# Sixteen stores taken off the load queue of a pooling and memory-attention layer: eight issued by POOL, eight by ACT

## The chip, the cores and the metric

The kernel runs on one core of one Trainium2 chip. The metric is the device time of one execution in microseconds (us). The engines of the core are PE (matrix products), DVE (vector), ACT (scalar functions), POOL (general purpose) and SP, which computes nothing and only issues transfers. ACT and POOL can issue transfers too. Each engine works through its own list of instructions strictly in order; engines wait for one another, and for transfers, by semaphores.

## The reference

One layer of a streaming encoder on 2048 tokens of width 1024, in float32:

```python
hn = rms_norm(h, norm_g[i])
mem_kv = jnp.einsum('bnd,de->bne', mem_n, w_mem_kv[i])
proj = jnp.einsum('bsd,de->bse', hn, pool_w_in[j])
u, mq, gate = jnp.split(proj, [POOL_WIDTH, POOL_WIDTH + MEM_WIDTH], axis=-1)
tok = multi_scale_pool(u, pool_w_group[j], pool_scale[j])      # windows 2, 4, 8, 16; then a 192x192 product per group
mem_o = memory_attention(mq, mem_k, mem_v)                     # 4 heads of 64, 256 memory rows
branch = jnp.concatenate([tok, mem_o], axis=-1) * jax.nn.silu(gate)
h = h + jnp.einsum('bse,ed->bsd', branch, w_out[i])
return rms_norm(h, final_norm_g)
```

## The kernel before, in words

Every float32 product is made of three products of a high and a low half: `_split` (L42 to L46) writes the high half by a cast (L38, mostly on ACT) and the low half by a subtraction (L46, on DVE), and `_mm3` issues the three matmuls (L51, L52, L53). A tile of weights can't be used by PE before both of its halves are made.

The 2048 tokens are four blocks of 512, taken as two pairs. For the first pair the input projection runs over tiles of 128 columns: `q` tiles (queries of the memory attention), `g` tiles (gates) and `z` tiles (pooling inputs), in the order of the list `TILES`. It begins with four query products, then gate tile 5. Between the products stand hooks: the fold (`fold`, hook 12), the loads and products of the memory keys and values (`load_memory`, `memory`), the row statistics of the second pair (`row_stats`), and four stages (`stage`) that prepare the second pair's inputs. Eighteen steps of the attention (`Attention.step`: scores L580 and L581, softmax L583 to L592, transposes L603, mix L615) are spread over the same stretch.

The fold multiplies the pooling weights into the input weights: for each of 8 row blocks k it loads 384 KB (`w_uT`, tile `raw`), PE makes the product, ACT copies it out of PSUM (L322) into a tile `zz`, and one transfer stores it to `w_z` in DRAM (L323), from where the `z` tiles are loaded later. `raw` tiles rotate through 4 buffers, `zz` tiles through 4.

`take_query` scales and splits each query product into `zz` and stores the two halves to `q_d` (L488); for the first pair that is 4 products with 2 stores each. `take_gate` puts a gate through Silu (L497) and stores it to `g_d`; ACT issues that store itself (L498).

All loads up to the second pair go through `load`, which keeps them in one order on SP:

```python
    def load(**kw):

        if not last:
            last.append(sp.dma_start(**kw))
        else:
            with tc.issue_after(last[-1].ins):
                last.append(sp.dma_start(**kw))
```

The order of each engine's list is worked out by a scheduler from a timeline of its own, so a store that moves to another engine can move other instructions as well. Transfers issued by SP and ACT take eight completion semaphores in turn (DMAHW0 to DMAHW7 in the lists below). A transfer may only be issued when the transfer that had its semaphore before it has landed; if it has not, the issuing engine stands still, and everything behind it on that engine too. Transfers issued by POOL have eight of their own (DMASW0 to DMASW7).

Of the kernel before, what the change touches and what calls it, by code (L numbers as in the profile page):

```python
# [8 lines left out]
F32 = mybir.dt.float32  # L9
# [32 lines left out]
def _split(nc, hi, lo, src, hi_eng, lo_eng="dve"):  # L42

    _cast(nc, hi_eng, hi, src)
    e = nc.gpsimd if lo_eng == "pool" else nc.vector
    return e.tensor_tensor(out=lo, in0=src, in1=hi.bitcast(F32), op=ALU.subtract)  # L46


def _mm3(nc, ps, ahi, alo, bhi, blo, start, stop, **kw):

    nc.tensor.matmul(ps, lhsT=ahi, rhs=bhi, start=start, stop=False, **kw)  # L51
    nc.tensor.matmul(ps, lhsT=ahi, rhs=blo, start=False, stop=False, **kw)  # L52
    nc.tensor.matmul(ps, lhsT=alo, rhs=bhi, start=False, stop=stop, **kw)  # L53
# [3 lines left out]
def trunk(ctx, tc, x, xT, mem, memT, norm_g, mem_norm_g, w_mem, w_out, w_in, w_uT, w_g, p_scale, final_g,  # L57
# [4 lines left out]
    nc = tc.nc  # L62
    sp = nc.sync
# [16 lines left out]
    def raw_tile(shape=(P, D)):  # L80
        return raw.tile(list(shape), F32, name="raw")
# [4 lines left out]
    def zz(shape, dt=F32):  # L86

        n = 1
        for v in shape[1:]:
            n *= v  # L90
        t = zw.tile([P, HALO + D], dt, name="zz")[:, :n]
        if len(shape) == 3:
            t = t.rearrange("p (a b) -> p a b", a=shape[1])
        return t
# [22 lines left out]
# [7 lines that stand above are left out]
        return last[-1]  # L124
# [170 lines left out]
    w_z = dram.tile([NJ, P, KT, P], F32, name="w_z")  # L295

    def fold():

        low = att.tile([P, D], F32R, name="ptl", bufs=1)[:, :4 * GD].rearrange("p (a l e) -> p a l e", a=2, l=2)
        tails = [[att.tile([P, 2, GD], F32R, name="pr") for _ in range(2)], [low[:, a] for a in range(2)]]  # L300
        for t in tails[0] + tails[1]:
            nc.vector.memset(t.bitcast(F32), 0.0)
        for l in range(2):
            r = slice(64 * l, 64 * l + 64)
            for a in range(2):
                _split(nc, tails[0][a][r, l, :], tails[1][a][r, l, :], wgb[r, a, :], "dve")
        for k in range(KT):
            wu = raw_tile((P, 6, P))
            load(out=wu, in_=w_uT[k])
            zs = zz((P, 6 * P))  # L310
            ut = ch.tile([P, 2, 2, P], F32R, name=("wh", "wl")[k % 2])
            nc.scalar.copy(ut[:, 0], wu[:, 4:6, :])
            nc.gpsimd.tensor_tensor(out=ut[:, 1], in0=wu[:, 4:6, :], in1=ut[:, 0].bitcast(F32), op=ALU.subtract)
            pss = [ps_mm.tile([P, 2, GD], F32, name="mm") for _ in range(2)]
            for a, ps in enumerate(pss):
                for l in range(2):
                    nc.tensor.matmul(ps[:, l, :], lhsT=wu[:, 2 * a + l, :], rhs=wga[:, 2 * a + l, :], start=l == 0,  # L317
                                     stop=False)
                _mm3(nc, ps, ut[:, 0, a, :], ut[:, 1, a, :], tails[0][a], tails[1][a], False, True)
            for a, ps in enumerate(pss):  # L320
                c = slice(2 * a * GD, 2 * (a + 1) * GD)
                nc.scalar.copy(zs[:, c], ps.rearrange("p l e -> p (l e)"))  # L322
            sp.dma_start(out=w_z[:, :, k, :].rearrange("j p f -> p j f"), in_=zs.rearrange("p (j f) -> p j f", j=6))  # L323

# [88 lines left out]
    q_d = [dram.tile([2, 2, P, 2, BT], F32, name=f"q_d{s}") for s in range(2)]  # L415
# [62 lines left out]
    def take_query(s, p0):  # L478
        def take(i, a, ps, op, rest):
            p = p0 + i  # L480
            src = ps
            if rest is not None:
                src = sgp.tile([P, BT], F32, name="sg")
                nc.vector.tensor_tensor(out=src, in0=ps, in1=rest, op=op)
            q = zz((P, 2, BT), F32R)
            _split(nc, q[:, 0, :], q[:, 1, :], src, "act")
            for i in range(2):
                sp.dma_start(out=q_d[s][p, i, :, a, :], in_=q[:, i, :].bitcast(F32))  # L488
        return take

    def take_gate(s, j):
# [278 lines left out]
    def norm(a):  # L770
        first_norm(a)
        for f in unscaled[a]:
            f()

    hooks = {7: [lambda: norm(0)], 10: [lambda: norm(1)], 12: [fold, lambda: ahead.append(load_tile(w_in[6], load)), lambda: loaded.extend(load_memory())],
             14: [lambda: load_memory_rest(loaded)],
             15: [lambda: memory_norm(loaded)], 17: [lambda: memory(loaded)], 19: [lambda: stats(0)], 21: [lambda: stats(1)]}
# [97 lines left out]
```

## Time and profile before

| | |
|---|---|
| time, median of 3 executions | 634.14 us (634.12 to 636.33) |
| time of the profiled execution | 636.03 us |
| span of the profiled execution, first to last instruction | 634.3 us |
| PE busy | 598.7 us, 94% of the span |
| DVE, ACT, POOL busy | 406.2, 324.9, 153.7 us |
| moved by the transfers | 124.41 MB, mean 196 GB/s |

The span is the part of the time that the trace divides among instructions; the profiled execution spent 1.7 us around it. PE is busy in all but some 36 us, so only what changes those, or the clock at which PE runs, can change the time by much.

### The profile page before, as it was taken

The page shows a single profiled execution, that of the slowest core. Times are in us where ns is not written, and L with a number is a line of the kernel's source. Part 1 is how long each engine was busy: PE and PEld are TensorE (multiplying, and loading weights), DVE is VectorE, ACT ScalarE, POOL GpSimd, SP SyncE. Part 2 cuts the span into 40 slices and gives each one's busy share as a digit, 9 for nine tenths or more (in the row PEclk, how much of TensorE's full clock was granted, in tenths as well). Part 3 has the DMA queues.
Part 4 walks back from the last instruction along what each step waited for, and adds up shares of the span by engine and source line. Part 5 has one row for each costly group of instructions (what it writes and reads, how often), then busy time and mean ns, then how long its engine had stood idle before and what let it go on. Part 6 is the DMA issues. An engine that isn't in the chain of part 4 may idle for free.

```text
span 634.3 us, 8389 instructions
## 1 busy us (share of the span) xinstructions
PE 598.7 (94%) x2846; PEld 496.6 (78%) x2846; DVE 406.2 (64%) x686; ACT 324.9 (51%) x672; POOL 153.7 (24%) x165
## 2 busy tenths in 40 slices
PE   7989779989989999999999999999999999999992
PEld 4879668868767888888888777877888888888882
DVE  6370247599785768896779756999864257515126
ACT  6825446346463664665864889644734234114112
POOL 0021123253451304100049200454000002107016
PEclk9999979989989999999999999999999999999997
DMA  8949995466464943667233434277991256940006
GB/s 315 398 158 337 395 352 158 116 208 216 158 240 149 314 152 124 224 218 238 92 101 97 168 110 144 60 231 252 389 405 63 65 187 218 359 167 0 1 0 265
DMA packets 54382, 124.41 MB, mean 196 GB/s; under 512 B 6722, under 2 KB 15682, under 8 KB 54340
## 3 DMA queue, kind: packets, MB, share of 16 engines
q1 hardware_dynamic: 45972, 106.57, 48.9%
q10 hardware_dynamic: 6832, 12.60, 5.3%
q0 software_dynamic: 1536, 4.72, 2.0%
q8 instruction: 22, 0.36, 0.2%
q14 instruction: 20, 0.16, 0.1%
HBM read 86.63 MB, written 36.70 MB: 194 GB/s over the span
## 4 chain that ended last, share of the span: by engine, by line
PE 62%; DVE 14%; DMA 7%; ACT 6%; POOL 5%; issue 4%; SPq 1%; ACTq 0%; POOLq 0%; DVEq 0%
PE mm L51 14%; PE mm L52 14%; PE mm L53 14%; POOL zz L522 4%; DMA raw<-in_xT 3%; PE sc L52 2%; PE sc L53 2%; PE pt L52 2%; PE pt L53 2%; PE pt L51 2%; PE sc L51 2%; DVE wl L46 2%; PE mm L317 2%; DVE raw L101 2%; DVE zz L531 1%
## 5 line engine op out<-in xcount | busy, mean ns | idle before, releaser
L51 PE MATMUL mm<-x,wh 128*128 128x512 f32 x480 | 190.9, 399 | 13.2 <-ACT wh L38 8.3
L52 PE MATMUL mm<-x,wh 128*128 128x512 f32 x480 | 189.5, 395 | 0.6 <-DVE x L229 0.6
L53 PE MATMUL mm<-x,wl 128*128 128x512 f32 x480 | 187.2, 394 | 0.0
L46 DVE TENSOR_TENSOR wl<-raw,wh 128x512 fp32r<-128x512 f32 x104 | 76.7, 741 | 110.8 <-ACT wh L38 110.5
L38 ACT CAST wh<-raw 128x512 fp32r<-128x512 f32 x104 | 63.7, 618 | 113.2 <-PE pt L53 80.5
L522 POOL TENSOR_TENSOR zz<-zz 128x527 f32<-128x527 f32 (+6 forms) x64 | 84.5, 1332 | 145.7 <-DVE zz L549 48.7
L51 PEld LDWEIGHTS mm<-x,wh 128*128 128x128 f32 x480 | 91.3, 190 | 34.5 <-ACT wh L38 9.2
L52 PEld LDWEIGHTS mm<-x,wh 128*128 128x128 f32 x480 | 91.2, 190 | 18.8 <-DVE x L229 1.2
L53 PEld LDWEIGHTS mm<-x,wl 128*128 128x128 f32 x480 | 91.1, 190 | 18.1
L51 PE MATMUL mm<-wh,x 128*128 128x512 f32 x128 | 49.7, 390 | 0.4 <-ACT sg L497 0.4
L53 PE MATMUL mm<-wh,x 128*128 128x512 f32 x128 | 49.8, 389 | 0.0
L52 PE MATMUL mm<-wl,x 128*128 128x512 f32 x128 | 49.8, 389 | 0.0
L674 POOL TENSOR_TENSOR rstdo<-sso,half 128x1 f32<-128x1 f32 x16 | 14.7, 919 | 129.5 <-DVE sso L716 129.5
L587 ACT ACTIVATE pr<-sc,nm 128x256 f32<-128x256 f32 x64 | 29.8, 471 | 24.9 <-DVE nm L583 23.0
L592 ACT ACTIVATE pr<-pr,rc 128x256 f32<-128x256 f32 x64 | 29.1, 504 | 19.9 <-DVE rc L590 19.2
L51 PEld LDWEIGHTS mm<-wh,x 128*128 128x128 f32 x128 | 24.0, 188 | 5.8 <-ACT sg L497 0.8
L53 PEld LDWEIGHTS mm<-wh,x 128*128 128x128 f32 x128 | 24.0, 188 | 5.0
L38 ACT CAST x<-raw 128x512 fp32r<-128x512 f32 x28 | 16.8, 619 | 21.7 <-DVE raw L266 13.9
L52 PEld LDWEIGHTS mm<-wl,x 128*128 128x128 f32 x128 | 24.0, 188 | 5.0
L46 DVE TENSOR_TENSOR x<-raw,x 128x512 fp32r<-128x512 f32 x28 | 23.6, 864 | 4.1 <-ACT x L38 3.9
L38 ACT CAST x<-zz 128x512 fp32r<-128x512 f32 x32 | 18.3, 618 | 13.5 <-DMA zz<-br_d 5.2
L583 DVE TENSOR_REDUCE nm<-sc 128x2 f32<-128x512 f32 x32 | 21.8, 682 | 5.2 <-PE sc L581 5.0
(180 smaller groups left out, 1049.8 us busy)
## 6 DMA issues: line engine op xcount, KB each, us to landing
raw<-in_w_in SPq DMA_DIRECT2D x19, 512.0 KB, 5.1
x<-in_x SPq DMA_DIRECT2D x16, 512.0 KB, 8.6
g_d<-sg ACTq DMA_DIRECT2D x32, 256.0 KB, 2.7
raw<-in_w_out SPq DMA_DIRECT2D x16, 512.0 KB, 4.5
raw<-w_z SPq DMA_DIRECT2D x12, 512.0 KB, 4.3
sg<-g_d SPq DMA_DIRECT2D x24, 256.0 KB, 3.7
br_d<-zz SPq DMA_DIRECT2D x12, 512.0 KB, 4.4
x<-in_xT SPq DMA_DIRECT2D x8, 512.0 KB, 7.7
```

Of the source, the lines that this page charges most:

```text
L38: return nc.scalar.copy(hi, src)
L46: return e.tensor_tensor(out=lo, in0=src, in1=hi.bitcast(F32), op=ALU.subtract)
L51: nc.tensor.matmul(ps, lhsT=ahi, rhs=bhi, start=start, stop=False, **kw)
L52: nc.tensor.matmul(ps, lhsT=ahi, rhs=blo, start=False, stop=False, **kw)
L53: nc.tensor.matmul(ps, lhsT=alo, rhs=bhi, start=False, stop=stop, **kw)
L101: return eng.tensor_tensor(out=o, in0=a, in1=b, op=ALU.subtract)
L317: nc.tensor.matmul(ps[:, l, :], lhsT=wu[:, 2 * a + l, :], rhs=wga[:, 2 * a + l, :], start=l == 0, stop=False)
L522: nc.gpsimd.tensor_tensor(out=cur[rows, c0:c1], in0=prev[rows, c0:c1], in1=prev[rows, c0 - step:c1 - step], op=ALU.add)
L583: nc.vector.tensor_reduce(out=nm, in_=ps, axis=AX.X, op=ALU.max, negate=True)
L587: nc.scalar.activation(out=pr[:, h, :], in_=ps[:, h, :], func=AF.Exp, bias=nm[:, h:h + 1], accum_out=su[:, h:h + 1])
L592: nc.scalar.mul(pr[:, h, :], pr[:, h, :], rc[:, h:h + 1])
L674: nc.gpsimd.tensor_tensor(out=ro, in0=sso[:, 1, t:t + 1], in1=half[:, :1], op=ALU.pow)
```

## The change

The stores of the fold (L323) are issued by ACT, and the query stores of the first pair (L488) by POOL. Both were issued by SP. The query stores of the second pair stay on SP.

```diff
@@ -320,7 +320,7 @@
             for a, ps in enumerate(pss):
                 c = slice(2 * a * GD, 2 * (a + 1) * GD)
                 nc.scalar.copy(zs[:, c], ps.rearrange("p l e -> p (l e)"))
-            sp.dma_start(out=w_z[:, :, k, :].rearrange("j p f -> p j f"), in_=zs.rearrange("p (j f) -> p j f", j=6))
+            nc.scalar.dma_start(out=w_z[:, :, k, :].rearrange("j p f -> p j f"), in_=zs.rearrange("p (j f) -> p j f", j=6))
@@ -485,7 +485,7 @@
             for i in range(2):
-                sp.dma_start(out=q_d[s][p, i, :, a, :], in_=q[:, i, :].bitcast(F32))
+                (sp if s else nc.gpsimd).dma_start(out=q_d[s][p, i, :, a, :], in_=q[:, i, :].bitcast(F32))
```

On SP, from the fourth fold load to the memory loads, the list of before was as follows (`raw<-in_w_uT` are the loads of the fold, `x_639` and `mq` take the memory, `x_644` its weights):

```order
L123 DMA raw<-in_w_uT 128x768 x4
L488 DMA q_d_174<-zz 128x512 x8
L123 DMA raw<-in_w_uT 128x768
L323 DMA w_z<-zz 128x6x128
L123 DMA raw<-in_w_uT 128x768
L323 DMA w_z<-zz 128x6x128
L123 DMA raw<-in_w_uT 128x768
L323 DMA w_z<-zz 128x6x128
L123 DMA raw<-in_w_uT 128x768
L323 DMA w_z<-zz 128x6x128
```

Of the changed kernel SP's list at that place, up to the weights of gate tile 3 (the second `raw<-in_w_in`) and the first rows for the statistics (`x_974<-in_x`), is:

```order
L123 DMA raw<-in_w_uT 128x768 x8
L123 DMA raw<-in_w_in 128x1024
L123 DMA x_639<-in_mem 128x1024 x2
L123 DMA mq<-in_memT 128x1024 x2
L123 DMA x_644<-in_w_mem 128x1024 x2
L123 DMA pth<-in_w_mem 128x1024
L123 DMA ptl<-in_w_mem 128x1024
L123 DMA raw<-in_w_in 128x1024
L123 DMA ci<-in_cinv 128x96
L123 DMA x_974<-in_x 128x1024 x2
```

Sixteen stores have left SP's list; the loads stand in the same order as before.

On ACT, between the gates of tile 4 (`sg_724` and `sg_728`) and the cast of the weights of gate tile 3 (`wh_736`), the list of before, with what each row waits for, was:

```order
L497 ACTIVATE sg_724<-sg_724 128x512 [waits DVE_49]
L368 ACTIVATE zz_753<-mq_146,gm_149 128x256 [waits DMAHW5_49,DMAHW1_49,Activation_49]
L368 ACTIVATE zz_753<-mq_146,gm_149 128x256 x3
L498 DMA g_d0_170<-sg_724 128x512 [waits DMAHW5_49,Activation_49]
L497 ACTIVATE sg_728<-sg_728 128x512 [waits DVE_49]
L498 DMA g_d0_170<-sg_728 128x512 [waits DMAHW0_49,Activation_49]
L38 CAST wh_736<-raw_732 128x512 [waits DMAHW4_49,Pool_49]
```

In the changed kernel the same place reads:

```order
L497 ACTIVATE sg_724<-sg_724 128x512 [waits DVE_49]
L498 DMA g_d0_170<-sg_724 128x512 [waits DMAHW3_49,Activation_49]
L368 ACTIVATE zz_753<-mq_146,gm_149 128x256 [waits DMAHW5_49,DMAHW1_49]
L368 ACTIVATE zz_753<-mq_146,gm_149 128x256 x3
L497 ACTIVATE sg_728<-sg_728 128x512 [waits DVE_49]
L498 DMA g_d0_170<-sg_728 128x512 [waits DMAHW7_49,Activation_49]
L38 CAST wh_736<-raw_732 128x512 [waits DMAHW4_49,Pool_49]
```

The second gate store stood behind DMAHW0 and now stands behind DMAHW7. SP's lists with their waits show who has each: in both kernels it is the second transfer of `x_974<-in_x`. The first gate store waited for the last fold store (DMAHW5) and now waits for `ptl<-in_w_mem` (DMAHW3).

The third place is on PE, at the transposes L603 of one attention step in the stretch of the stages. Of before:

```order
L615 MATMUL sc<-ptl,vhl 128x256
L52 MATMUL mm<-x_265,wh 128x512
L53 MATMUL mm<-x_264,wl 128x512
L603 MATMUL pt<-ident,pr 128x128 x4
L51 MATMUL mm<-x_176,wh 128x512
```

and of the changed kernel:

```order
L615 MATMUL sc<-ptl,vhl 128x256
L51 MATMUL mm<-x_176,wh 128x512
L52 MATMUL mm<-x_177,wh 128x512
L603 MATMUL pt<-ident,pr 128x128 x4
L53 MATMUL mm<-x_176,wl 128x512
```

These transposes stand two large matmuls further down the projection than before. Shifts of one to eleven such matmuls are found at most attention steps behind the fold.

## Rows read from the trace of the kernel before

**Rows 1.** The page's head and part 1: busy us (share of the span) xinstructions.
```profile
span 634.3 us, 8389 instructions
PE 598.7 (94%) x2846; PEld 496.6 (78%) x2846; DVE 406.2 (64%) x686; ACT 324.9 (51%) x672; POOL 153.7 (24%) x165
```

**Rows 2.** Timeline of PE, 74 to 89 us: start, us, what [idle before <-releaser].
```profile
74.82 0.39 PE L53 MATMUL mm<-x,wl 128*128 128x512 f32 x1
83.47 0.80 PE L51 MATMUL mm<-x,wh 128*128 128x512 f32 x1 [8.27 <-ACT wh L38]
```

**Rows 3.** Chain that ended last, 74 to 84 us: start, us, what.
```profile
74.29 8.01 DMA x<-in_x
...
82.38 0.33 ACTq L498
```

**Rows 4.** Timeline of ACT, 79 to 83 us.
```profile
79.77 0.33 ACTq L498 DMA_DIRECT2D g_d<-sg  x1
80.14 0.63 ACT L497 ACTIVATE sg<-sg 128x512 f32<-128x512 f32 x1 [3.05 <-DMA w_z<-zz]
...
82.80 0.62 ACT L38 CAST wh<-raw 128x512 fp32r<-128x512 f32 x1 [2.04 <-DMA x<-in_x]
```

**Rows 5.** Stretches: PE, PEld, DVE, ACT, POOL busy (xcount), PEclk, DMA share, GB/s.
```profile
39.00:45.20 6.20, 6.20 (x33) 5.28 (x32) 2.78 (x7) 0.71 (x2) 0.00 (x0) 1.00 0.11 42
46.00:64.00 18.00, 18.00 (x110) 18.00 (x109) 2.14 (x4) 10.61 (x23) 2.93 (x4) 1.00 1.03 342
64.00:75.20 11.20, 11.20 (x50) 8.95 (x48) 3.23 (x8) 5.30 (x12) 1.98 (x4) 1.00 1.06 396
75.20:82.30 7.10, 0.01 (x1) 0.00 (x0) 0.69 (x1) 2.52 (x6) 0.55 (x1) 0.70 1.05 405
83.50:88.20 4.70, 4.70 (x14) 4.02 (x15) 4.08 (x8) 4.09 (x8) 0.00 (x0) 0.50 1.01 329
```

**Rows 6.** Timeline of SP, 28 to 77 us: start, us to the end of the last issue.
```profile
33.98 13.07 SPq L488 DMA_DIRECT2D q_d<-zz  x8
47.40 0.33 SPq L123 DMA_DIRECT2D raw<-in_w_uT  x1
...
71.20 0.40 SPq L323 DMA_DIRECT2D w_z<-zz  x1
...
73.67 2.84 SPq L123 DMA_DIRECT2D x<-in_x  x4
```

**Rows 7.** What SP waited for, 30 to 98 us: total, times, longest.
```profile
SPq L323 <- ACT zz L322: 5.1, 5, 1.9
...
SPq L123 <- PE mm L317: 0.3, 1, 0.3
```

**Rows 8.** The instructions on the tile w_z, 46 to 76 us: ns min/median/max, first and last start.
```profile
L323 SPq DMA_DIRECT2D w_z<-zz x8: 370/420/1179, 49.7 to 71.2; - x8
```
**Rows 9.** Transfers issued from 46 to 82.3 us: xcount, size, median us to landing.
```profile
w_z<-zz SPq DMA_DIRECT2D x8, 384.0 KB, 7.3
```

**Rows 10.** Timeline of POOL, at the fold and at a store of 256 KB later on.
```profile
51.90 0.73 POOL L313 TENSOR_TENSOR wh<-raw,wh 128x256 fp32r<-128x256 f32 x1 [13.40 <-ACT wh L312]
...
127.47 0.61 POOL L279 DMA_DIRECT2D xs_d<-raw  x1 [0.85 <-DVE raw L266]
```

**Rows 11.** Timeline of PE: the first row behind four of its idle times, 138 to 201 us.
```profile
139.01 0.38 PE L615 MATMUL sc<-ptl,vhl 128*128 128x256 f32 x1 [2.69 <-DVE ptl L46]
...
160.74 0.39 PE L615 MATMUL sc<-ptl,vhl 128*128 128x256 f32 x1 [0.35 <-DVE ptl L46]
...
184.02 1.11 PE L603 MATMUL pt<-ident,pr 128*128 128x128 f32 x4 [2.83 <-ACT pr L592]
...
200.94 0.38 PE L615 MATMUL sc<-ptl,vhl 128*128 128x256 f32 x1 [0.93 <-DVE ptl L46]
```

**Rows 12.** Stretches behind two of them, columns as in rows 5.
```profile
139.00:142.80 3.80, 3.79 (x14) 3.31 (x15) 2.92 (x6) 1.47 (x3) 0.00 (x0) 0.56 0.81 252
...
183.80:187.20 3.40, 3.18 (x10) 2.59 (x11) 3.40 (x5) 2.98 (x6) 2.60 (x3) 0.50 0.64 167
```

## The prediction

> **What bounds the kernel now.** I began with the page: a span of 634.3 us with PE busy for 598.7 of them [rows 1]. A change of transfers can only pay where PE stands idle or runs slowly, so the next view was PE's timeline. Its longest stop lies just behind the edited code: the last matmul of gate tile 4 starts at 74.82 and takes 0.39, the next one starts at 83.47 after 8.27 us without work [rows 2]. The reader should see in that row that the releaser is ACT's cast of the weights of gate tile 3 (L38).
>
> Why is ACT late? The chain of waits [rows 3] and ACT's timeline [rows 4] answer it. ACT issued the first gate store of tile 4 at 79.77, having stood idle for most of the 3.05 us ahead of the Silu at 80.14, which the profile puts down to a store of the fold; it issued the second gate store at 82.38, and only then came the cast, at 82.80. The second gate store waited for a transfer of `x<-in_x` that was issued at 74.29 and took 8.01, so it landed at 82.30. That wait is not for data. The store reuses the completion semaphore of that transfer, as the list of ACT ahead shows.
>
> Why does that transfer land so late? The stretches [rows 5] show it: from 39 to 45.2 us the transfer engines are used to 0.11, but from 46 to 82.3 us the share is 1.03 to 1.06 in each stretch. Everything that lands in these 36 us lands when its turn comes. SP issued ahead of that all along: the fold's stores took a median of 7.3 us from issue to landing [rows 9], for 384 KB that need about 1.0 us at the 396 GB/s of 64 to 75.2 [rows 5].
>
> After the stop PE runs at a granted clock of 0.50, the 1.2 GHz level, until 88.2 [rows 5]: 4.70 us of which half, 2.35, is lost. The next idle times lie between 126 and 202 us. Those of 2.69 at 139.01 and 2.83 at 184.02 [rows 11] are followed by stretches at 0.56 and 0.50 [rows 12]; behind those of 0.35 and 0.93 the trace has no slow stretch.
>
> **The change part by part.**
>
> *Query stores leave SP.* SP spent 13.07 us, from 33.98 on, on eight of them, mostly waiting for their data, and issued the fifth fold load at 47.40 [rows 6]. It looks as if the loads could start 13 us sooner. They can't: the fifth fold load needs the `raw` buffer of the first, which PE reads only when it begins the fold, and after the query stores SP still waited 0.3 us for PE's matmul L317 [rows 7]. The compiled list of the changed kernel has the four L317 rows of a fold block ahead of its other matmuls, so the buffer comes free somewhat sooner. I allow the load 0.3 to 0.7 us; the engines are empty then (0.11), so up to that much could pass to everything behind. I take 0.3.
>
> *Query stores on POOL.* A store of 256 KB costs POOL 0.61 us at 127.47 [rows 10]; eight cost 4.9. POOL stood idle for 13.40 us before its first fold subtraction behind the fourth block, at 51.90 [rows 10], so they are hidden, the four early ones (from about 35 us) in the 10 us before PE begins the fold. Without that cover POOL's subtractions, and with them PE, would be up to 2.4 us late (four stores), which the stop at 75 would absorb.
>
> *Fold stores leave SP.* That frees eight issues of 0.42 (3.4 us [rows 8]) and 5.1 us of waiting for ACT's copies [rows 7], 8.5 us together. SP will run ahead of where it was, but it feeds a set of engines that is full. From 46 us on the bytes ahead of the transfer that ends the stop are the same ones: the fold's loads and stores, the memory, its weights, gate tile 3. The last fold store was issued at 71.20 on SP [rows 6], ahead of it already. So I take 0 for this part, with a gain of 8.27 + 2.35 = 10.6 as the far bound, if the whole stop went.
>
> The Trainium skill says the same against the change in its page DMA: Bandwidth & Descriptors, section Issuing engines are not separate DMA queues: transfers of all issuing engines run on the same 16 engines, and issuing from several only saves issue time. By that rule alone the gain would be the issue time, 3.4 us; by the shares above, it is nothing, since SP's issue time is not what the landing waits for.
>
> *Fold stores on ACT.* Eight issues at 0.33 (a gate store, [rows 4]) to 0.42 make 2.6 to 3.4 us more on ACT. ACT is busy for 10.61 of the 18 us from 46 to 64 and 5.30 of 11.2 after that [rows 5], so it has 13 us of room, and PE's products have four PSUM buffers. ACT may also stand still for a semaphore: the sixth store waits for the weights of tile 4 to land, which the cast behind it needs anyway. I take 0. If the cover fails, PE's fold or gate tile 4 slips; PE has to wait until 83 all the same, so the first 8 us of that cost nothing.
>
> *What the stop waits for afterwards.* ACT's list still has the second gate store ahead of the cast, and it still waits for the same second `x_974` transfer. The first gate store now waits for `ptl<-in_w_mem`, four transfers earlier. It will therefore be sent sooner and share the engines with the two `x_974` transfers: 256 KB at 405 GB/s [rows 5] is up to 0.65 us. I take 0.2, since only part of it falls ahead of the landing. So PE goes on at 83.47 - 0.3 + 0.2, about 83.4.
>
> *What moves behind.* The scheduler moved the transposes and mixes of most attention steps one to eleven large matmuls down. At 184.02 the shift is two matmuls; a large one takes about 0.23 us, as 48 of them in 11.2 us show [rows 5], so that stop of 2.83 may lose 0.45; at 160.74 the mix is six further down, which covers the 0.35 [rows 11]. I take 0.5 as a gain; the order behind 200 us differs more and I give it nothing, with 1.5 either way.
>
> **The sum.** 0.1 + 0.5 = 0.6 us less: a profiled execution of 636.03 would become 635.4. That execution lies 1.9 above the median of the runs shown, 634.14; applied to the median the forecast is 633.5. I count within 0.5%, 3.2 us, as no change, which is about what a measurement of this kernel can tell.
>
> **The rivals.**
>
> A. *The loads do come forward.* For it: SP waited 5.1 us for the fold's copies, and with them gone its issues lie earlier. If the landing moved by those 5.1 us, PE would go on at 78.4. The clock of 0.70 over the 7.1 us of the stop [rows 5] says it fell for the last 4.3 of them, at about 78.0, so the slow stretch would remain: 634.14 - 5.1 = 629.0. Against it: the share of 1.03 and more from 46 us on. It decides by that share alone: if some of it is not bytes but gaps between transfers of one queue, a second queue fills them.
>
> B. *The stores on their own queue take turns with the loads.* Then the first gate store (0.65) and a fold store that still runs (384 KB at 405 GB/s, 0.97) go ahead of the `x_974` transfers: 1.6 us later, 635.2 with the gain of 0.5 behind. The Trainium skill has this rule, in the same page, section Queues, rings and completion order: each engine goes round its queues packet by packet. No row shows more than one busy queue for long here.
>
> C. *One more stop like those at 139 and 184.* An order that puts a transpose or a mix where DVE or ACT is 2.7 us behind costs 2.69 and, over the 3.80 us at 0.56 [rows 12], another 1.7: 4.4 more, 634.14 - 0.1 + 4.4 = 638.4. For it: both stops come from such an order, and a share of the rows there is new. Against: the shifts that I found lie downwards, which gives DVE and ACT more time. It decides at an idle time between 0.93, which has no slow stretch, and 2.69, which has one.
>
> D. *One of these two stops goes.* The mirror image: 184.02 loses 1.9 of its 2.83 and with it the slow stretch (half of 3.40, 1.7): 3.6, to 630.5.
>
> **Chances and range.** The forecast has 0.50, A 0.13, B 0.13, C 0.12, D 0.12. The forecast and B end within 0.5%, but the unknown order behind 200 us can carry some of them over either edge, 0.02 to each side. Faster: A, D and 0.02, with the part of A and D that stays within the bound taken off (0.02), 0.25. Slower: C and 0.02, 0.14. The same: 0.61. The range leaves out C and the deeper half of A: 628.8 to 637.0. The likeliest case has a range of its own from its bounds: 633.5 - 0.4 (the load) - 1.5 (the order) = 631.6, and 633.5 + 0.3 + 0.45 (the gate store) + 1.5 = 635.8.
>
> **What would show it.** Right: PE's stop ends between 82.5 and 84 us, with the releaser ACT L38 and ACT's second gate store waiting for `x<-in_x`; the share from 46 to 82 us is still 1.0 or more; the fold stores land in under 7.3 us; POOL's issues lie before 48 us, and none of PE's idle times names POOL there. Wrong: a stop at 75 us that is shorter than 7 us or ends with another releaser; idle time of PE between 46 and 64, which would mean that ACT's stores hold its copies up; or a changed number of stretches at half clock from 126 to 202 us, which would carry the difference in place of the stores.

## The result, and the profile after

| | before | changed |
|---|---|---|
| time, median of 4 executions each, taken together | 635.24 us (634.12 to 637.13) | 641.57 us (640.44 to 643.02) |
| ratio to before, 95% interval | 1 | 1.0102 (1.0078 to 1.0127) |
| span of the profiled execution | 634.3 us | 640.2 us |

The change makes the kernel 1.0% slower, outside the range that was forecast. The page of the changed kernel has the same work as [rows 1] but for two table loads more on ACT, some 3 us more of PE's busy time, and 3 us more in which PE stands idle:

```profile
span 640.2 us, 8398 instructions
PE 601.8 (94%) x2846; PEld 499.6 (78%) x2846; DVE 413.2 (65%) x686; ACT 327.5 (51%) x674; POOL 155.6 (24%) x173
```

PE's timeline of the changed kernel, the rows that begin behind a longer idle time (in brackets, with what ended it):

```profile
68.84 0.80 PE L51 MATMUL mm<-x,wh 128*128 128x512 f32 x1 [3.79 <-ACT wh L38]
84.07 0.50 PE L51 MATMUL mm<-x,wh 128*128 128x512 f32 x1 [2.53 <-ACT wh L38]
...
136.43 0.39 PE L615 MATMUL sc<-ptl,vhl 128*128 128x256 f32 x1 [1.61 <-DVE ptl L46]
159.61 0.39 PE L615 MATMUL sc<-ptl,vhl 128*128 128x256 f32 x1 [2.65 <-DVE ptl L46]
181.76 0.44 PE L603 MATMUL pt<-ident,pr 128*128 128x128 f32 x2 [2.05 <-ACT pr L592]
216.73 0.83 PE L603 MATMUL pt<-ident,pr 128*128 128x128 f32 x4 [1.80 <-ACT pr L592]
...
348.58 0.58 PE L615 MATMUL sc<-ptl,vhl 128*128 128x256 f32 x1 [2.36 <-DVE ptl L46]
427.19 0.80 PE L51 MATMUL mm<-x,wh 128*128 128x512 f32 x1 [2.83 <-DVE u L104]
```

The stop of 8.27 at the edited place [rows 2] is now two, 3.79 and 2.53, and those of [rows 11] have their answers at 136, 160 and 182. How the edited place divides differs between executions: three kernels further down that have the same lists up to there (two_places, three_moves, old_order_behind_600) show 1.80 and 7.42, 1.62 and 5.97, 3.50 and 3.42. What before does not have are the three last rows. Each of them is followed by a stretch at half the clock, as these windows of the changed kernel show (the column that reads 0.50 is PE's granted clock; 1.2 of 2.4 GHz):

```profile
218.84:222.25 3.41, 3.41 (x12) 2.93 (x12) 2.86 (x5) 1.48 (x3) 0.48 (x1) 0.50 0.32 126
348.54:351.95 3.41, 3.37 (x14) 3.18 (x14) 3.41 (x6) 1.79 (x4) 2.20 (x2) 0.50 0.91 287
427.05:430.46 3.41, 3.27 (x8) 2.62 (x9) 2.48 (x5) 0.00 (x0) 0.00 (x0) 0.50 0.70 243
```

To see where the time goes, the large matmuls (rows of L51 to L53 that write `mm`) are counted in PE's timeline of each kernel, and their start times compared at equal counts. The 600th starts at 206.78 before and at 202.81 in the changed kernel: up to there, the edited place included, the profiled execution of the changed kernel is 4.0 ahead. The 900th starts at 285.55 and 285.89, the 1470th at 445.42 and 451.03. So 4.3 are lost from the 600th to the 900th, where the stop at 216.73 lies, and 5.3 from the 900th to the 1470th, where the other two lie. The first loss is largely one of this execution: two_places and three_moves have the same lists up to the 900th, show 0.33 and 0.34 at the place of the stop at 216.73, and lose 1.5 and 1.3 there. No store that was moved is in either stretch.

DVE explains the last two stops. Its timeline in the changed kernel:

```profile
343.02 0.69 DVE L104 TENSOR_TENSOR u<-mm,u 128x512 f32<-128x512 f32 x1
343.62 1.39 DVE L46 TENSOR_TENSOR wl<-raw,wh 128x512 fp32r<-128x512 f32 x1
344.94 2.98 DVE L537 SCALAR_TENSOR_TENSOR zz<-zz,psc,sg 128x512 f32<-128x512 f32 x2
347.85 0.68 DVE L46 TENSOR_TENSOR ptl<-pt,pth 128x512 fp32r<-128x512 f32 x1
...
424.19 2.22 DVE L537 SCALAR_TENSOR_TENSOR zz<-zz,psc,sg 128x512 f32<-128x512 f32 x2
426.45 0.69 DVE L104 TENSOR_TENSOR u<-mm,u 128x512 f32<-128x512 f32 x1
```

and the same instructions in the kernel before:

```profile
342.72 0.68 DVE L46 TENSOR_TENSOR ptl<-pt,pth 128x512 fp32r<-128x512 f32 x1
343.32 2.39 DVE L537 SCALAR_TENSOR_TENSOR zz<-zz,psc,sg 128x512 f32<-128x512 f32 x2
...
421.88 0.69 DVE L104 TENSOR_TENSOR u<-mm,u 128x512 f32<-128x512 f32 x1
422.49 1.81 DVE L537 SCALAR_TENSOR_TENSOR zz<-zz,psc,sg 128x512 f32<-128x512 f32 x2
```

PE waits for `ptl` in the one place and for `u` in the other. Before, each stands ahead of the two pooling rows L537; in the changed kernel it stands behind them.

At the edited place the engines were as full as forecast (a share of 0.98 from 46 to 64 us, 1.00 to 75.2 and 1.01 to 83), but the landings moved apart. The transfer view of 46 to 74 us of the changed kernel (count, size, median us from issue to landing):

```profile
w_z<-zz ACTq DMA_DIRECT2D x8, 384.0 KB, 11.5
...
mq<-in_memT SPq DMA_DIRECT2D x2, 512.0 KB, 6.1
x<-in_w_mem SPq DMA_DIRECT2D x2, 512.0 KB, 6.3
```

and of the same stretch before:

```profile
w_z<-zz SPq DMA_DIRECT2D x8, 384.0 KB, 7.3
...
mq<-in_memT SPq DMA_DIRECT2D x2, 512.0 KB, 9.5
x<-in_w_mem SPq DMA_DIRECT2D x2, 512.0 KB, 10.6
```

On a queue of their own the fold's stores land later (7.3 to 11.5) and the loads sooner. The late stores then hold up both issuers: SP for the completion semaphore of the fold store that was issued at 54.39 and took 12.9 to land, and ACT's copy for the `zz` buffer of the same store, the fourth ahead of its own. SP of the changed kernel, and ACT:

```profile
59.39 8.29 SPq L123 DMA_DIRECT2D mq<-in_memT  x2
```

```profile
67.41 0.86 ACT L322 COPY zz<-mm 128x384 f32<-128x384 f32 x2 [4.34 <-DMA w_z<-zz]
68.16 0.63 ACT L38 CAST wh<-raw 128x512 fp32r<-128x512 f32 x1
```

SP needs 8.29 us for two issues, and the cast of tile 4's weights stands behind ACT's wait of 4.34, hence PE's new stop at 68.84. It does not decide the time: in the four kernels with these lists PE goes on behind the second stop at 84.07, 84.62, 82.67 and 83.68, whichever of the two stops is the longer.

### The profile page after: what moved, and what is told of

Its sections match the earlier page's. It is cut to its first block, busy times and chain, and to the rows that moved or that the text cites. A ratio compares the mean times of both kernels' runs of the same rounds, so it can differ in the third digit from the quotient of the medians.

```text
span 640.2 us, 8398 instructions
## 1 busy us (share of the span) xinstructions
PE 601.8 (94%) x2846; PEld 499.6 (78%) x2846; DVE 413.2 (65%) x686; ACT 327.5 (51%) x674; POOL 155.6 (24%) x173
## 4 chain that ended last, share of the span: by engine, by line
PE 64%; DVE 14%; DMA 9%; ACT 8%; issue 3%; POOL 1%; ACTq 0%; SPq 0%; POOLq 0%; DVEq 0%
PE mm L51 15%; PE mm L52 15%; PE mm L53 15%; PE sc L53 2%; PE pt L53 2%; PE pt L52 2%; PE sc L52 2%; PE sc L51 2%; PE pt L51 2%; DMA w_z<-zz 2%; DVE zz L537 2%; DVE wl L46 2%; DMA o_d<-pr 2%; DVE x L46 2%; DMA raw<-in_xT 2%
## 5 line engine op out<-in xcount | busy, mean ns | idle before, releaser
L51 PE MATMUL mm<-x,wh 128*128 128x512 f32 x480 | 191.3, 401 | 12.7 <-ACT wh L38 6.3
L53 PE MATMUL mm<-x,wl 128*128 128x512 f32 x480 | 188.6, 397 | 0.0
L46 DVE TENSOR_TENSOR wl<-raw,wh 128x512 fp32r<-128x512 f32 x104 | 79.6, 769 | 111.2 <-ACT wh L38 89.9
L51 PEld LDWEIGHTS mm<-x,wh 128*128 128x128 f32 x480 | 92.1, 192 | 33.7 <-ACT wh L38 7.4
L522 POOL TENSOR_TENSOR zz<-zz 128x527 f32<-128x527 f32 (+6 forms) x64 | 80.9, 1275 | 152.1 <-DVE wl L46 46.0
L52 PEld LDWEIGHTS mm<-x,wh 128*128 128x128 f32 x480 | 92.5, 193 | 18.5 <-DVE x L229 0.5
L53 PEld LDWEIGHTS mm<-x,wl 128*128 128x128 f32 x480 | 92.0, 192 | 18.1
L53 PE MATMUL mm<-wh,x 128*128 128x512 f32 x128 | 49.6, 389 | 0.0
L51 PE MATMUL mm<-wh,x 128*128 128x512 f32 x128 | 49.6, 389 | 0.0
L592 ACT ACTIVATE pr<-pr,rc 128x256 f32<-128x256 f32 x64 | 29.0, 502 | 17.7 <-DVE rc L590 17.5
L53 PEld LDWEIGHTS mm<-wh,x 128*128 128x128 f32 x128 | 24.0, 188 | 5.0
L51 PEld LDWEIGHTS mm<-wh,x 128*128 128x128 f32 x128 | 24.0, 188 | 5.0
L46 DVE TENSOR_TENSOR x<-raw,x 128x512 fp32r<-128x512 f32 x28 | 24.8, 909 | 3.9 <-ACT x L38 3.7
L603 PE MATMUL pt<-ident,pr 128*128 128x128 f32 x128 | 21.7, 284 | 4.9 <-ACT pr L592 4.9
```

The source lines that it names most:

```text
L522: nc.gpsimd.tensor_tensor(out=cur[rows, c0:c1], in0=prev[rows, c0:c1], in1=prev[rows, c0 - step:c1 - step], op=ALU.add)
L592: nc.scalar.mul(pr[:, h, :], pr[:, h, :], rc[:, h:h + 1])
L603: nc.tensor.transpose(ps[:, 2 * h + kt, :], pr[:, h, kt * P:(kt + 1) * P], ident)
```

## The experiments

The theory after the result: **order**. The scheduler drew another order for all engines, and that order costs; the stores themselves gain or cost little. The rival: **queues**. The late fold stores, and the issuers that wait for them, cost.

The lists of a kernel can be held: every instruction gets an edge to the one that stands ahead of it in a recorded list of its engine, so the scheduler has no choice. Only the sixteen stores are left free.

```diff
+def hold_order(tc):
...
+    at = {i.name: i for i in tc.nc.cur_bb.bb.instructions}
+    for row in json.loads(zlib.decompress(base64.b85decode(ORDER))):
+        row = [at[f"I-{n}"] for n in row]
+        for a, b in zip(row, row[1:]):
...
+            tc.add_manual_dep(b, a.name, mybir.DependencyInfo(mybir.DependencyClass.NoSync, mybir.DependencyReason.DATA), reason="order")
...
         trunk(tc, **aps)
+        hold_order(tc)
```

**New queues, old order.** The changed kernel with this edit, `ORDER` taken from the kernel before.

> The stores are issued by POOL and ACT as in the changed kernel; every other instruction of each engine is held in the order of the kernel before. Theory 'order': the loss is in the order behind 200 us, which the scheduler changed, and the stores themselves gain. At PE's 582nd large matmul the changed kernel was 4.2 us ahead of before (196.73 against 200.94), so this one should be about 4 us faster than before, 630 to 633, without the long stops at 217, 349 and 427. Theory 'queues': the stores on the new queues cost the time (late fold stores, semaphores); then this one is as slow as the changed kernel, 639 to 643.

Measured: 634.12 us, ratio 0.9997 (0.9984 to 1.0011). The loss is gone, and so is the gain that I expected beside it. PE's timeline has neither of the two late stops:

```profile
83.32 0.79 PE L51 MATMUL mm<-x,wh 128*128 128x512 f32 x1 [6.91 <-ACT wh L38]
...
354.17 0.50 PE L51 MATMUL mm<-x,wh 128*128 128x512 f32 x1 [1.35 <-ACT sg L497]
...
420.94 0.50 PE L51 MATMUL mm<-x,wh 128*128 128x512 f32 x1 [0.19 <-DVE u L104]
```

**Old queues, new order.** The kernel before with the same edit, `ORDER` taken from the changed kernel.

> All sixteen stores stay on SP; every other instruction of each engine is held in the order of the changed kernel. Theory 'order': the stops at 217, 349 and 427 are here too, and the early gain of the stores is not, so as slow as the changed kernel or slower, 641 to 647. Theory 'queues': as the kernel before, 633 to 637.

Measured: 638.54 us, ratio 1.0075 (1.0056 to 1.0095). Not one store is moved, and three quarters of the loss are there, with the two stops:

```profile
349.78 0.39 PE L615 MATMUL sc<-ptl,vhl 128*128 128x256 f32 x1 [2.35 <-DVE ptl L46]
...
428.22 0.50 PE L51 MATMUL mm<-x,wh 128*128 128x512 f32 x1 [2.83 <-DVE u L104]
```

With the changed kernel and before, these two make a square: the order costs 0.75% on the old queues and 1.05% on the new ones; the queues change nothing in the old order, and 0.27 points in the new, where the two intervals overlap. So the order is what costs. Whether the queues cost a little beside the new order is not resolved.

**Each half of the change alone**, with the scheduler free:

```diff
-                sp.dma_start(out=q_d[s][p, i, :, a, :], in_=q[:, i, :].bitcast(F32))
+                (sp if s else nc.gpsimd).dma_start(out=q_d[s][p, i, :, a, :], in_=q[:, i, :].bitcast(F32))
```

> Only the query stores move, to POOL. The lists of PE and DVE come out the same as in the changed kernel, so they are the part that changed the order. Theory 'order': 641 to 647, with the late stops. Theory 'queues': the fold stores on ACT landed up to 13 us after issue and are the suspects there; without them 633 to 637.

Measured: 639.35 us, ratio 1.0074 (1.0046 to 1.0103). Its lists of PE and DVE are those of the changed kernel, row for row, and it has the stops (2.36 at 345.91, 2.84 at 424.61). One of its seven executions took 633.52, the others 638.98 to 641.87; what the one had otherwise is not known.

```diff
-            sp.dma_start(out=w_z[:, :, k, :].rearrange("j p f -> p j f"), in_=zs.rearrange("p (j f) -> p j f", j=6))
+            nc.scalar.dma_start(out=w_z[:, :, k, :].rearrange("j p f -> p j f"), in_=zs.rearrange("p (j f) -> p j f", j=6))
```

> Only the fold stores move, to ACT. PE's list differs from that of before in 77 rows, not in 3115. Theory 'order': the stop at 75 us (8.27 us and a slow stretch of 10.24 us before) splits as in the changed kernel and nothing is lost behind, 630 to 633. Theory 'queues': the late fold stores cost what the changed kernel lost, 639 to 643.

Measured: 633.03 us, ratio 0.9979 (0.9965 to 0.9993). So the fold stores on ACT, with the order drawn for them, gain 0.2%, and the query stores on POOL brought the order that costs.

**The same two stores on other engines** tell whether POOL or ACT as such matters. The query stores on ACT, alone (`nc.scalar` in place of `nc.gpsimd` above):

> Only the query stores move, to ACT in place of POOL, and the scheduler orders freely. Its lists keep the order of the kernel before (9 rows of PE's differ), where the move to POOL changed 186. Theory 'order': no loss, 632 to 636, and no stops of over 2 us near 348 and 427. Theory 'queues': SP without the query stores loses as it did with them on POOL (639.4 then), 637 to 641.

Measured: 634.35 us, ratio 1.0009 (0.9995 to 1.0023), no late stop (0.19 at 421.41). And the fold's stores on POOL, alone (`nc.gpsimd` in place of `nc.scalar`):

> Only the fold stores move, and to POOL; the query stores stay on SP, and the scheduler orders freely. It draws a third order up to PE's 830th large matmul (about 265 us); from the 839th on the attention rows stand where they stand in the changed kernel (mixes at 839, scores at 942), with the pooling rows L537 ahead of ptl and of u. Theory 'the late order costs, whatever drew it': behind 280 us it loses the 5 to 6 us that the other kernels with this order lost there (5.6, 5.4 and 4.3), with stops near 348 and 427, and takes 636 to 641. Theory 'the query stores on POOL cost': no such loss, 632 to 636.

Measured: 637.77 us, ratio 1.0061 (1.0042 to 1.0080). The query stores are untouched in this kernel, and PE's timeline shows the two stops nearly to the hundredth:

```profile
345.23 0.39 PE L615 MATMUL sc<-ptl,vhl 128*128 128x256 f32 x1 [2.36 <-DVE ptl L46]
422.96 0.50 PE L51 MATMUL mm<-x,wh 128*128 128x512 f32 x1 [2.84 <-DVE u L104]
```

**Which rows of the order.** The changed kernel with its own order held, but for two rows of DVE:

```diff
+L46 TENSOR_TENSOR ptl_3159<-pt_3269,pth_3158 128x4x128
 L537 SCALAR_TENSOR_TENSOR zz_3182<-zz_3182,psc_151,sg_3169 128x512
 L537 SCALAR_TENSOR_TENSOR zz_3182<-zz_3182,psc_151,sg_3171 128x512
-L46 TENSOR_TENSOR ptl_3159<-pt_3269,pth_3158 128x4x128
...
+L104 TENSOR_TENSOR u_4109<-mm_4096,u_4053 128x512
 L537 SCALAR_TENSOR_TENSOR zz_4020<-zz_4020,psc_151,sg_4010 128x512
 L537 SCALAR_TENSOR_TENSOR zz_4020<-zz_4020,psc_151,sg_4012 128x512
-L104 TENSOR_TENSOR u_4109<-mm_4096,u_4053 128x512
```

> The changed kernel with every list held in its own order, but for two places on DVE, where one row goes ahead of two pooling rows L537 as it stands in the kernel before: the subtraction L46 of ptl (its pt had been cast at 338.2, it ran at 347.85) and the addition L104 of u (ran at 426.45, behind 2.22 of L537). Theory 'order at single places': the stops of 2.36 at 348.58 and 2.83 at 427.19 shrink to under 0.6 and take their slow stretches of 3.41 with them, 2 x (2 + 1.7), so 7 to 8 us faster than the changed kernel and near the kernel before, 633 to 636. Theory 'order as a whole': the wait comes back at the next step, and the time stays within 2 us of the changed kernel's 641.6.

Measured: 637.99 us, ratio 1.0066 (1.0041 to 1.0090), between the two theories: 0.36 points of the 1.02 are back, at the edge of what is resolved, since the interval still overlaps that of the changed kernel (from 1.0078). PE's timeline:

```profile
349.58 0.73 PE L603 MATMUL pt<-ident,pr 128*128 128x128 f32 x3 [1.55 <-ACT pr L592]
...
426.28 0.50 PE L51 MATMUL mm<-x,wh 128*128 128x512 f32 x1 [0.57 <-DVE u L104]
```

The second stop went, as expected (2.83 to 0.57). The first only passed to the next row that was held up, ACT's scaling L592, whose reciprocal L590 also stood behind the two L537. So a third move:

```diff
 L46 TENSOR_TENSOR ptl_3159<-pt_3269,pth_3158 128x4x128
+L590 RECIPROCAL rc_3265<-su_3262 128x2
 L537 SCALAR_TENSOR_TENSOR zz_3182<-zz_3182,psc_151,sg_3169 128x512
 L537 SCALAR_TENSOR_TENSOR zz_3182<-zz_3182,psc_151,sg_3171 128x512
-L590 RECIPROCAL rc_3265<-su_3262 128x2
```

> As the changed kernel with two rows of DVE moved (638.0), and a third: the reciprocal L590, which ran at 348.84 behind the two pooling rows L537 and for which ACT's scaling and PE's transposes at 349.58 waited, goes ahead of them too. Theory 'single rows': the stop of 1.55 at 349.58 goes, 1.5 us less, 636 to 637. Theory 'the order as a whole': the 1.5 us come back in the steps behind, 638.

Measured: 636.24 us, ratio 1.0039 (1.0025 to 1.0053). Three moved rows have given back 0.63 of 1.02 points, some 4 us. The effect of the third alone isn't resolved, since the interval overlaps that of two moves, and its stop has passed on once more, to 1.87 at 348.13, behind another row of DVE:

```profile
348.13 0.50 PE L51 MATMUL mm<-x,wh 128*128 128x512 f32 x1 [1.87 <-DVE u L104]
```

**Where the order begins to cost.** The changed kernel with its own order up to PE's 600th large matmul and that of before behind it, held as above:

> The stores on their new queues; the lists of the changed kernel up to PE's 600th large matmul (at 202.81 us), the order of the kernel before behind it. Theory 'the loss lies behind 200 us': at the 600th the changed kernel was 4.0 us ahead of before and 1.1 ahead of the kernel with the new queues and the old order, which took 634.1, so 632 to 634. If the new order already costs something ahead of 200 us that only shows later, 636 or more.

Measured: 632.65 us, ratio 0.9974 (0.9961 to 0.9987). The whole loss lies behind the 600th. The same with the fold's stores on POOL, its own order up to the 841st and that of before behind it:

> Fold stores on POOL, with the order that the scheduler drew for it up to PE's 841st large matmul and the order of the kernel before behind it. With its own order throughout it took 637.8; in its trace it was 2.9 us ahead of before from 240 to 340 us and lost it behind. Theory 'the cost begins behind the 841st': the 2.9 stay, 630 to 633. If it takes 635 or more, the late order was not what cost.

Measured: 632.96 us, ratio 0.9981 (0.9967 to 0.9995), against 1.0061 with its own order to the end: there the loss lies behind the 841st. Both kernels beat before and the changed one.

**One engine's order alone.** PE's list of the changed kernel among the other lists of before, on the new queues, and the reverse:

> The stores on their new queues; PE's list held in the order of the changed kernel, all other lists in the order of the kernel before. If the loss is carried by where DVE's rows stand (pooling rows ahead of what PE needs), it is largely gone: 633 to 636. If it is carried by where PE's transposes and mixes stand, it stays: 638 to 642. A list that fits the others less well may also cost more than either.

> The mirror of the one ahead: PE's list in the order of the kernel before, all other lists in that of the changed kernel, the stores on their new queues. DVE's rows as the carrier: 638 to 642. PE's rows as the carrier: 633 to 636.

Measured: 653.33 us, ratio 1.0304 (1.0280 to 1.0327), and 661.99 us, ratio 1.0436 (1.0412 to 1.0459). Neither theory, but what the first expectation added: each mixture is far worse than either order. The lists of one drawing fit together, and the question which engine's list carries the loss has no answer of this kind.

**The stop at the edited place.** The prediction held that a semaphore of the gate store, not the weights, sets its end. The kernel before, held, with one row of ACT moved:

```diff
 L497 ACTIVATE sg_724<-sg_724 128x512
+L38 CAST wh_736<-raw_732 128x512
 L368 ACTIVATE zz_753<-mq_146,gm_149 128x256 x4
 L498 DMA g_d0_170<-sg_724 128x512
 L497 ACTIVATE sg_728<-sg_728 128x512
 L498 DMA g_d0_170<-sg_728 128x512
-L38 CAST wh_736<-raw_732 128x512
```

> The kernel before, all stores on SP and all lists held, but for one row on ACT: the cast of the weights of gate tile 3 (L38) goes ahead of the four rows L368, the gate stores L498 and the second Silu. Theory 'a semaphore, not data, sets the end of PE's stop': the weights landed at 78.52, so the cast runs at once and PE goes on at 79.1 to 79.6 in place of 83.47, 4 us less, and some of the slow stretch of 10.24 goes too: 628 to 631. Rival 'the bytes': something else of tile 3 or of what follows lands only at 82 to 84 and PE stops again within the next 5 us; 633 to 635.

Measured: 634.35 us, ratio 1.0000 (0.9985 to 1.0015). The reading of the stop was right, and the gain was nothing, a time in the rival's range. PE goes on at 79.23 in place of 83.47, and stops again 14 us later:

```profile
79.23 0.79 PE L51 MATMUL mm<-x,wh 128*128 128x512 f32 x1 [4.07 <-ACT wh L38]
93.25 0.80 PE L53 MATMUL sc<-zz,wl 128*128 128x256 f32 x2 [3.34 <-DVE wl L46]
```

What is late then can be read backwards. DVE's subtraction for PE ran at 92.50 (at 92.24 before, so no sooner), behind a row that waited 6.03 for ACT's statistics; ACT's timeline shows why they were late:

```profile
87.75 0.33 ACTq L498 DMA_DIRECT2D g_d<-sg  x1
88.12 1.06 ACT L220 ACTIVATE x<-x 128x1024 f32<-128x1024 f32 x1 [5.98 <-DMA mq<-q_d]
```

It is the same second gate store, with other work behind it now. It does not wait for the same transfer: the semaphores were handed out anew with the moved row, and the store has that of the `mq<-q_d` issued at 78.50, which took 9.2 and landed at 87.7, in place of the `x<-in_x` that landed at 82.30 before. So this run shows that the gate store's semaphore held up the cast, but not what the cast's move alone would gain.

**Three moves in the old order.** New queues and old order, with the same cast moved, and two more rows:

```diff
 # DVE
+L46 TENSOR_TENSOR ptl_1128<-pt_1211,pth_1127 128x4x128
 L46 TENSOR_TENSOR x11_1236<-raw_1251,x10_1235 128x512
-L46 TENSOR_TENSOR ptl_1128<-pt_1211,pth_1127 128x4x128
 # ACT
+L592 ACTIVATE pr_1578<-pr_1578,rc_1582 128x256 x2
 L497 ACT_TABLE_LOAD
 L497 ACTIVATE sg_1620<-sg_1620 128x512
 L498 DMA g_d0_170<-sg_1620 128x512
 L38 CAST x10_1235<-raw_1863 128x512
-L592 ACTIVATE pr_1578<-pr_1578,rc_1582 128x256 x2
```

> The stores on their new queues, the old order held, with three rows moved on DVE and ACT: the same cast ahead of the gate stores, ptl's subtraction ahead of the subtraction of x that took 4.32 us at 133.64, and the scaling L592 ahead of the table load and Silu at 179.23. Theory 'order at single places': the stop at 83.3 ends 4 us sooner, those at 138.6 and 182.6 (2.66 and 2.85) shrink to under 1 and lose their slow stretches of 3.41; 4 + 3.9 + 3.6 = 11.5 less than the 634.1 of this kernel without the three moves, 622 to 626. Theory 'order as a whole': half or more of it returns at the next steps, 628 to 634.

Measured: 633.40 us, ratio 0.9988 (0.9973 to 1.0003); the 11.5 us are not there. The stops that were aimed at did go (2.85 at 182.64 became 0.25 at 181.67), and others came: 1.94 at 94.67, 1.82 at 190.05. (A stop of 3.10 at 69.06 lies ahead of all three moved rows and so isn't of their making.) Ahead of 200 us, waits that were taken away brought no gain in either kernel. Full transfer engines are not the whole reason: in the trace of before their share is 0.98 to 1.06 from 46 to 96 us, but 0.41 to 0.71 from there to 200. What else took the time back is not shown.

All kernels together, sorted by which order stands behind the 900th matmul (us from the 900th to the 1470th in the profiled execution, read as above):

| kernel | ratio | 900th to 1470th |
|---|---|---|
| before | 1 | 159.87 |
| new_queues_old_order | 0.9997 | 159.91 |
| fold_alone | 0.9979 | 159.88 |
| q_on_act | 1.0009 | 159.92 |
| old_order_behind_600 | 0.9974 | 159.91 |
| third_order_to_841 | 0.9981 | 159.97 |
| cast_first | 1.0000 | 160.18 |
| three_places | 0.9988 | 160.19 |
| changed | 1.0102 | 165.14 |
| q_alone | 1.0074 | 165.31 |
| old_queues_new_order | 1.0075 | 164.16 |
| fold_on_pool | 1.0061 | 162.67 |
| two_places | 1.0066 | 163.65 |
| three_moves | 1.0039 | 162.12 |

Eight kernels with the order of before take 159.9 to 160.2 there, whatever their queues; with the new order it is 2.3 to 5.4 more. The stretch ahead of the 900th can't be read so finely from one profile each: three kernels that are the same up to there (changed, two_places, three_moves) reach it at 285.89, 285.89 and 282.58.

The same stretch, 900th to 1470th, by busy time (before, changed, old_queues_new_order, three_moves; columns as in [rows 5]):

```profile
285.55:445.42 159.87, 156.67 (x768) 129.15 (x766) 125.90 (x194) 106.83 (x219) 49.53 (x38) 1.00 0.46 151
285.89:451.03 165.14, 158.77 (x768) 131.83 (x766) 130.75 (x194) 106.61 (x220) 47.74 (x38) 0.98 0.45 147
286.39:450.55 164.16, 156.94 (x767) 129.12 (x766) 130.58 (x194) 106.40 (x219) 45.57 (x38) 1.00 0.44 149
282.58:444.70 162.12, 156.31 (x768) 129.13 (x766) 130.31 (x194) 106.56 (x220) 47.19 (x38) 1.00 0.43 149
```

PE stands idle there for 3.2, 6.4, 7.2 and 5.8 us (the length less its busy time), and of the four only the changed kernel has slow clock in it, with 2.1 us more busy time than before. Three_moves takes 3.0 us less there than the changed kernel, 2.5 of it busy time and 0.6 idle time. That its stretch has no slow clock may or may not be due to the moves, since old_queues_new_order has none either, with both stops. DVE needs 4.4 to 4.9 us more for the same 194 instructions in the new order, with or without the moves.

## Why the prediction was wrong

**The step that failed** is "What moves behind", in its words "the order behind 200 us differs more and I give it nothing, with 1.5 either way". It measured 4.3 to 5.4 us from the 900th to the 1470th matmul in the three kernels with exactly that order (changed, q_alone, old_queues_new_order), and 0.75% (0.56 to 0.95) of the whole time with the queues left alone, 4.8 us. The step looked at PE's list and the stretch of 126 to 202 us, where the shifts lay downwards. Behind it they do not: counted in PE's timelines, the transposes and mixes stand 0 to 11 large matmuls further down ahead of the 600th, but from 32 further up to 5 further down behind the 900th. The three rows whose moves gave back 0.63 of the 1.02 points stand on DVE's list, near 345 and 424: there `ptl`, a reciprocal and `u` went behind two pooling rows, which no count of shifted matmuls shows.

**Rival C** had the mechanism right and its place wrong. It was "an order that puts a transpose or a mix where DVE or ACT is 2.7 us behind", once, for 638.4, with a chance of 0.12. Such stops came three times in the profiled execution, of 1.80, 2.36 and 2.83, each with a slow stretch; the last two come with the order, in old_queues_new_order, q_alone and fold_on_pool as well. The gain ahead of the 600th paid for a part, 0.26% by old_order_behind_600. The price of 4.4 for each was too high: both together measured 4.3 to 5.4. The chance rested on looking for them in one stretch only.

**The start of the loads and the gate store** (-0.3 and +0.2): PE goes on at 83.32 with the new queues in the old order, and at 84.07 in the changed kernel, where 83.4 was forecast. For the kernel before, the cause, a gate store that waits for its semaphore, is shown by the moved cast. In these two executions another cause gave nearly the same end, which is luck. In the changed kernel the `x<-in_x` transfer landed at 82.39, but the second gate store was issued at 82.96, behind its Silu of 82.30: the stop at 68.84, which the forecast didn't have, had made tile 4 late. With the new queues in the old order ACT's rows ahead of that Silu waited 3.59 for a fold store. In three_moves and old_order_behind_600 the store did wait for `x<-in_x`, and PE went on at 82.67 and 83.68.

**Fold stores, "I take 0 for this part"**: the sum held (0.9979 alone), and its reasons half. The engines stayed full, so rival A did not occur. But the stores were to land in under 7.3 us, and took 11.5. Turn-taking, rival B's mechanism, fits that, with the loads as its winners; it is not separated from SP's own waits, which left fewer loads under way. The Trainium skill has it in its page DMA: Bandwidth & Descriptors, section Queues, rings and completion order: each DMA engine goes round its queues packet by packet. The later landings of 11.5 agree with it. What B priced, 1.6 us at the stop, did not follow: the transfer that the second gate store waits for landed at 82.39, and at 82.30 before. The part *Fold stores on ACT* missed that late landings hold the four `zz` buffers; its fallback, that a late tile 4 costs nothing up to 83, is nearly what happened.

**Query stores on POOL**: hidden, as forecast, and no idle time of PE names POOL there. They cost through the order that came with them: on ACT, with nearly the order of before, the same stores cost nothing.

Of the signs given, the stop shorter than 7 us and the idle time of PE ahead of 64 (0.35 at 62.44) came true in the changed kernel, and neither carries the loss. The share of 1.0 or more was missed by little (0.98 from 46 to 64). The slow stretches from 126 to 202 us went from two to one; the three that carry part of the loss lie behind the window that was named.

The forecast of 633.5 was thus one for the moved stores in the order of before, which measured 634.12 (0.9997). What stays open: what in the scheduler's timeline made it draw this order for stores on POOL and not for the same stores on ACT, and which rows cause the 0.39% that are left after three moved rows; by the windows above they are idle time of PE, 2.6 us of it from the 900th to the 1470th. The stop at 216.73, which ACT's wait for a transfer `o_d<-pr` led to, is in the changed kernel's trace alone (q_alone has 0.67 there, with the same lists of PE and DVE); its part of the loss isn't separated. "Order" here takes in the semaphores, which are handed out with it.

## What to carry to other kernels

Where a scheduler sets the order, an edit of a few transfers is also a new drawing of every engine's list: compare the lists to the end of the program, on DVE and ACT as well as PE, and look for rows that PE waits for and that have passed behind long ones. To cost or to measure an edit by itself, hold the order of before; to keep a gain, hold the better order, part by part but for all engines at once. Do not price a single wait at its length. Ahead of 200 us the moves gave nothing here, since other waits came; behind 340 us three moved rows gave back some 4 us, where the first two alone had been expected to give 7 to 8.

## What was not expected of the hardware

**DVE beside POOL.** Two rows L537 cost 2.98 at 344.94, and 1.81 to 3.00 at the other places with POOL rows beside them, while one alone at 205.40 took 0.74, as DVE's timeline of before shows:

```profile
205.40 0.74 DVE L537 SCALAR_TENSOR_TENSOR zz<-zz,psc,sg 128x512 f32<-128x512 f32 x1
```

POOL of the changed kernel was busy all through the first:

```profile
342.41 8.33 POOL L522 TENSOR_TENSOR zz<-zz 128x525 f32<-128x525 f32 x6 [1.23 <-DVE zz L531]
```

In the same 8 us the subtraction L46 of `wl` took 1.39 in place of 0.68, and the addition L104, which reads `mm` in PSUM, its usual 0.69. At 133.64 a subtraction with three POOL rows beside it (3.51 from 133.89 in the new queues with the old order) took 4.32. The Trainium skill has the rule in its page SBUF — State Buffer, section SBUF: two separate sides: DVE instructions with two inputs in SBUF and POOL instructions that read SBUF lock each other out for a whole instruction. The rows agree; the one of 4.32 waited through three POOL rows. It makes the wrong order dearer: what stands behind L537 waits for POOL as well. How much of DVE's 4.4 to 4.9 us more behind the 900th comes from this was not measured.

**The slow clock is not bound to the length of a stop.** The stops of 2.36 and 2.83 in the changed kernel were followed by windows at 0.50; the same two stops with the old queues and the new order, 2.35 and 2.83, by windows at 1.00:

```profile
349.80:353.20 3.40, 3.40 (x20) 3.06 (x21) 3.40 (x5) 1.79 (x4) 2.50 (x4) 1.00 0.95 322
428.20:431.60 3.40, 3.38 (x15) 2.84 (x16) 2.68 (x5) 0.55 (x1) 0.00 (x0) 1.00 0.67 240
```

So the prediction's bound for a slow stretch, an idle time between 0.93 and 2.69, does not hold as a rule: a stop of 2.83 had none, and in the changed kernel the stop of 1.80 had one while that of 2.05 at 181.76 had none.
